# A hybrid diffusion block: the large GpSimd additions move to VectorE, and the inter-block weight is loaded instead of formed

## The chip, the cores and the metric

The kernel runs on one core of one Trainium2 chip, as one launch. The metric is device time in microseconds (us). The core has five instruction streams that run side by side and meet at semaphores: TensorE (PE in the profile; PEld is its weight load), VectorE (DVE), ScalarE (ACT), GpSimd (POOL) and SyncE (SP), which here issues nearly all DMA transfers. The order of instructions on each engine is fixed when the kernel is built: a scheduler takes the code's order as priority and puts out one list for each engine, so a change in the code can move rows far from it.

## What is computed

A sequence of 1024 latent tokens (width 1024), with 256 context tokens ahead of it as a prefix, goes through two kinds of recurrent heads in both directions, an output projection with a residual, and an expert-choice mixture of experts. Three parts of the reference matter for the change:

```python
# HGRN2 (4 heads): the key is 1 - f for each direction d
hg_k=[_to_heads(1.0 - f[:, :, d], HG_HEADS) for d in range(2)]

# mLSTM q and k: a 3x3 depthwise convolution over the 16 x 64 grid, then SiLU
y = lax.conv_general_dilated(t.reshape(B, rows, GRID_W, C), w[:, :, None, :], (1, 1), 'SAME', ...)
return jax.nn.silu(y + conv_b)

# mLSTM in chunks: weights within the chunk, and of the state that comes in
m_row = jnp.maximum(inter, jnp.max(d, axis=-1))
w_inter = jnp.exp(inter - m_row)
qk = jnp.einsum('bhid,bhjd->bhij', qc, kc) * jnp.exp(d - m_row[..., None])
num = jnp.einsum('bhij,bhjv->bhiv', qk, vc) + w_inter[..., None] * jnp.einsum('bhid,bhdv->bhiv', qc, c)
```

After the mixer, `v = rms_norm(xm) * (1 + scale) + shift` goes to the router and the experts. All arithmetic is float32 (products on TensorE are formed from two halves, high and low).

## The kernel before

The work is laid out in stages along the span. Until 215 us come the modulation, the context and HGRN2's values and gates; until some 460 us the four HGRN2 heads; until some 660 us output gates, the convolution, mLSTM values and the backward states; until some 900 us the eight blocks of 128 tokens of mLSTM outputs, mixer and router; then a sort that picks the tokens, and from 940 us the sixteen experts.

**HGRN2 (L640 to L711).** A head has two halves of 512 tokens. Features are on the partitions. L674 adds the two directions' keys on GpSimd (128x512, eight times); L347 on TensorE multiplies that sum with the queries; L675 forms the scaled queries of both directions on VectorE, and L363 scales the keys in the tree of levels.

**Convolution (L812 to L830).** A row r of 128 channels is one call of `conv(r)`, eight in all. L818 copies the projection into a padded tile, L821 forms the middle tap on ScalarE, L824 multiplies taps 3 and 5 on ScalarE and L825 adds each to the accumulator `cacc` on GpSimd. Six taps follow as L827 on VectorE. `silu2` (L502, L503) ends it, and the store to `d_qk` is issued by SP. Between these stand `back_k` (L842: load of keys, L480 to L486: transposed and scaled by `wkx`), `back_u` (L496 on TensorE, L386 on VectorE, store L853) and the modulation's sums (L295, L297), in the order of a list written out in the code:

```python
ORD = (5, 4, "v004", 6, "v044", 7, "v104", 0, "v144", "k7", 1, "u7", "k6", "k5", "u6", "k4", 2, "u5", 3,
       "o004", "u4", "k3", "o044", "u3", "k2", "u2", "o104", "k1", "M", "u1", "S0", "O0", "L0", "S1", "o144")
```

**Blocks (L932 to L952 and L1130 to L1180).** `scores(cc)` runs two blocks ahead of the mixer. SP loads `qkx` and then `MB` (L936): -M for eight head-directions, 128 numbers each, spread to all 128 partitions, 512 KB in 1024 pieces. Tiles `MB`, `E` and `qkx` have two buffers each. L943 (ScalarE, eight instructions) adds g to it and writes `E`; L944 (VectorE) takes the minimum with the causal mask; L945 is the exponent. GpSimd adds mu to `MB` in place (L946), ScalarE takes its exponent (L947), VectorE multiplies it with the queries (L950), and E with the scores from TensorE (L949). `outputs` (L957 to L982) uses both as stationary operands (L975 with E, L976 with MB). `mixed` loads `kin` and `go` (L1001, L1002) and forms `mix` (L1005, L1006). `mixer` loads `xm` (L1020), and L1027, L1028 add the residual. `router` forms the normalised row `vt`: L1052 to L1054, and L1055 adds the shift B2b on GpSimd (128x1024, eight times).

**Gates (`ml_gates`, L425 to L470).** It forms -M in one 128x128 tile and stores its two halves to `d_nm` in DRAM; `mu_b` is the copy of mu for L946, and `mcol` holds mu for each partition of that tile.

Of the kernel before, what the change touches and what calls it, by code (L numbers as in the profile page):

```python
# [9 lines left out]
F32 = mybir.dt.float32  # L10
# [5 lines left out]
AF = mybir.ActivationFunctionType  # L16
# [3 lines left out]
P = 128  # L20
# [12 lines left out]
def tile_hybrid_block(ctx, tc, x, c, cx, c_ctx, ada_w, ada_b, norm1_w, w_in, conv_w, conv_b,  # L33
# [6 lines left out]
    V, S, G, T = nc.vector, nc.scalar, nc.gpsimd, nc.tensor  # L40
# [12 lines left out]
    d_sb = dram.tile([8, P, 516], F32, name="d_sb")  # L53
    d_gx = dram.tile([16, 1024], F32, name="d_gx")
    d_nm = dram.tile([8, 1024], F32, name="d_nm")
    d_g = dram.tile([4, 1024], F32, name="d_g")
    d_v = dram.tile([1024, 1024], F32, name="d_v")
    d_acc = dram.tile([1024, 1024], F32, name="d_acc")
# [330 lines left out]
    def ml_gates(pool):  # L389
# [64 lines left out]
        V.tensor_scalar(M, M, -1.0, None, op0=OP.mult)  # L454
        for d in range(2):
            load(d_nm[4 * d:4 * d + 4].rearrange("h (c i) -> (h c) i", i=P), M[64 * d:64 * d + 32])
        pt = bank("ms")
        T.transpose(pt[:, 0:128], g, ident)
        T.transpose(pt[:, 128:256], b, ident)
# [3 lines left out]
        for d in range(2):  # L463
            V.tensor_copy(gT[:, :, d, :], xcol(0, d))
            S.activation(emn[:, :, d, :], xcol(128, d), AF.Exp, scale=-1.0)
            V.tensor_copy(mu_b[:, :, d, :], xst(0, d))
            V.tensor_sub(wkx[:, :, d, :], xcol(0, d), xst(80, d))
            V.tensor_sub(wsx[:, :, d, :], xst(0, d), xst(80, d))
            V.tensor_sub(wkc[:, :, d, :], view(pt, 64 * d + 32, [[1, 2], [2, 4]]), cst(80, d))
            V.tensor_sub(wsc[:, :, d, :], cst(0, d), cst(80, d))  # L470
# [105 lines left out]
    mlc = const.tile([P, 2, 4, 129], F32, name="mlc", tag="mlc", bufs=1)  # L576
    gT = const.tile([P, 8, 2, 4], F32, name="gT")
    emn = const.tile([P, 8, 2, 4], F32, name="emn")
    mu_b = const.tile([P, 8, 2, 4], F32, name="mu_b")
    wkx = const.tile([P, 8, 2, 4], F32, name="wkx")  # L580
    wsx = const.tile([P, 8, 2, 4], F32, name="wsx")
    wkc = const.tile([P, 2, 2, 4], F32, name="wkc")
# [65 lines left out]
    with tc.tile_pool(name="hgp", bufs=1) as hp_:  # L648
        tl = lambda name, shape, bufs: hp_.tile([P] + shape, F32, name=name, tag=name, bufs=bufs)
        fw = {}  # L650
        for h in range(4):
# [17 lines left out]
            for hf in range(2):  # L669
                f, qk = F[hf], QK[hf]  # L670
                K, Q = tl("hgK", [2, 512], 2), tl("hgQ", [2, 512], 3)
                A, U = tl("hgA", [4, P], 3), tl("hgU", [4, 2, P], 3)
                V.tensor_scalar(K, f, -1.0, 1.0, op0=OP.mult, op1=OP.add)
                G.tensor_add(qk[:, 1, :], K[:, 0, :], K[:, 1, :])  # L674
                V.tensor_mul(Q, qk[:, 0, :].unsqueeze(1).to_broadcast([P, 2, 512]), view(f, 512, [[-512, 2], [1, 512]]))  # L675
                dec = hg_tree(hp_, f, K, Q, qk, A)
                hg_u(hp_, K, lambda cc: hv[:, 4 * hf + cc, h * P:(h + 1) * P], U, ((0, 4 - hf), (1 - hf, 4)))
                Qs.append(Q), As.append(A), Us.append(U), decs.append(dec)
# [133 lines left out]
    def conv(r):  # L812
# [6 lines left out]
        acc = cvp.tile([P, 16, 64], F32, name="cacc", tag="cacc", bufs=2)  # L819
        tap = lambda t: view(pad, 65 * (t // 3) + t % 3, [[65, 16], [1, 64]])  # L820
        S.activation(acc, tap(4), AF.Identity, bias=convb[:, r:r + 1], scale=tapw(4, r))  # L821
        for t in (3, 5):
            one = cvp.tile([P, 16, 64], F32, name="cone", tag="cone", bufs=2)
            S.mul(one, tap(t), tapw(t, r))  # L824
            G.tensor_add(acc, acc, one)  # L825
        for t in (0, 1, 2, 6, 7, 8):
            V.scalar_tensor_tensor(acc, tap(t), tapw(t, r), acc, op0=OP.mult, op1=OP.add)  # L827
        res = cvp.tile([P, 1024], F32, name="cres", tag="cres", bufs=2)
        silu2(res, acc.rearrange("p r c -> p (r c)"))
# [101 lines left out]

    def scores(cc):  # L932

        qk, MB = tl("qkx", [8, P], 2), tl("MB", [8, P], 2)
        load(qk, d_qk[cc])
        load(MB, bass.AP(tensor=d_nm.tensor, offset=d_nm.offset + cc * P, ap=[[0, P], [1024, 8], [1, P]]))  # L936
        pq = bank("hg", [P, 4, P])
        for h in range(4):
            T.matmul(pq[:, h, :], qk[:, 4 + h, :], qk[:, h, :], start=True, stop=True)
        E = tl("E", [2, 4, P], 2)  # L940
        for d in range(2):
            for h in range(4):
                S.activation(E[:, d, h, :], MB[:, 4 * d + h, :], AF.Identity, bias=gT[:, cc, d, h:h + 1])  # L943
            V.tensor_tensor(E[:, d], E[:, d], cmask[:, d, :].unsqueeze(1).to_broadcast([P, 4, P]), op=OP.min)  # L944
        S.activation(E, E, AF.Exp)  # L945
        G.tensor_add(MB, MB, mu_b[:, cc].rearrange("p d h -> p (d h)").unsqueeze(2).to_broadcast([P, 8, P]))  # L946
        S.activation(MB, MB, AF.Exp)  # L947
        for d in range(2):
            V.scalar_tensor_tensor(E[:, d], pq, KSCALE, E[:, d], op0=OP.mult, op1=OP.mult)  # L949
            V.tensor_mul(MB[:, 4 * d:4 * d + 4, :], qk[:, 0:4, :], MB[:, 4 * d:4 * d + 4, :])  # L950
        kt = ml_k_tok(blk, lambda h: qk[:, 4 + h, :], wkx[:, cc, 0], False) if cc < 7 else None
        return E, MB, kt  # L952

# [93 lines left out]
    def router(cc, xm):  # L1047

        row = slice(cc * P, (cc + 1) * P)
        r2 = tb("r2", [1], 2)  # L1050
        vt = tb("vt", [1024])
        S.activation(vt, xm, AF.Square, scale=1.0 / 32, accum_out=r2)  # L1052
        rsqrt(r2, r2, 1)
        V.scalar_tensor_tensor(vt, xm, r2, A2b, op0=OP.mult, op1=OP.mult)  # L1054
        G.tensor_add(vt, vt, B2b)  # L1055
        kept["v"] = load(d_v[row], vt)
        if dbg and "xm" in dbg:
            nc.sync.dma_start(dbg["xm"][row], xm)
            nc.sync.dma_start(dbg["v"][row], vt)
        return r2  # L1060
# [389 lines left out]
```

## Time and profile before

| | |
|---|---|
| runs | 1557.04, 1558.73, 1561.94 us |
| median of the runs | 1558.73 us |
| the profiled execution, own time | 1559.33 us |
| the profiled execution, span of the core | 1557.6 us |
| PE, DVE, ACT, POOL busy | 1447.8, 1230.4, 864.7, 174.8 us |
| granted clock of TensorE, mean | 0.967 |
| chain that ended last | PE 64%, DVE 13%, DMA 10%, issue 6%, ACT 4%, POOL 2% |

The span is the stretch from the first to the last instruction of the core; the device time of the same execution is 1.7 us longer. A busy engine is not yet a bound: which wait ends last in a stage has to be read there. The chain of waits is followed back from the end, at each step to what released it. A timeline row gives the start, the length, the engine, the line, and in square brackets the idle time ahead of it with its releaser.

### The profile page before, as it was taken

To read this page: it belongs to the slowest core of one execution; us is meant where nothing else is said; L and a number is where in the kernel's file an instruction comes from. 1 tells how busy PE (TensorE), PEld (TensorE's weight loads), DVE (VectorE), ACT (ScalarE), POOL (GpSimd) and SP (SyncE) were. 2 spreads that over 40 slices of the span, in tenths; PEclk is the share of its full clock that TensorE was granted. 3 is DMA by queue.
4 is the path that set the end of the run, shared out by engine and by line. 5 is a ranking of instruction groups with operands and counts; after the bars stand their busy time and mean duration, and the time that the engine had idled before them with its cause. 6 is when DMAs were issued, how large, how long until landed. Compare 5 with 4: busy or idle time off the path is not lost.

```text
span 1557.6 us, 23134 instructions
## 1 busy us (share of the span) xinstructions
PE 1447.8 (93%) x8121; PEld 1206.9 (77%) x8121; DVE 1230.4 (79%) x2193; ACT 864.7 (56%) x1454; POOL 174.8 (11%) x136
## 2 busy tenths in 40 slices
PE   7999999999999998988888947999999999999996
PEld 2899878888898896977677735888888888888764
DVE  3685577888866859546757796999999999998887
ACT  3764424334434343345545315777787787777775
POOL 0000000000002221210222110010000000000003
PEclk9999999999999998989898977999999999999998
DMA  9741311220334254276753486999999999999942
GB/s 268 258 128 31 110 54 35 75 82 22 115 102 142 82 149 149 72 194 211 223 183 112 158 320 211 370 391 374 386 387 384 385 389 383 387 376 362 352 141 109
DMA packets 181201, 337.31 MB, mean 217 GB/s; under 512 B 13560, under 2 KB 108348, under 8 KB 181084
## 3 DMA queue, kind: packets, MB, share of 16 engines
q1 hardware_dynamic: 176472, 319.99, 58.0%
q0 software_dynamic: 4320, 15.73, 4.1%
q8 instruction: 64, 1.05, 0.3%
q14 instruction: 53, 0.43, 0.1%
q10 hardware_dynamic: 292, 0.10, 0.0%
HBM read 303.38 MB, written 32.39 MB: 216 GB/s over the span
## 4 chain that ended last, share of the span: by engine, by line
PE 64%; DVE 13%; DMA 10%; issue 6%; ACT 4%; POOL 2%; SPq 0%; ACTq 0%; POOLq 0%; DVEq 0%
PE mm L1303 22%; PE mm L278 11%; PE hg L1303 10%; PE mm L286 5%; PE hg L350 3%; DMA MB<-d_nm 3%; DVE cacc L827 3%; PE hg L215 2%; PE ms L1288 2%; DMA wraw<-in_w_in_dram 1%; PE mm L1026 1%; PE ms L382 1%; POOL cacc L825 1%; DMA wraw<-in_ada_w_dram 1%; PE mm L496 1%
## 5 line engine op out<-in xcount | busy, mean ns | idle before, releaser
L286 PE MATMUL mm<-whi,uh 128*128 128x256 f32 (+1 forms) x512 | 145.6, 284 | 3.0 <-DVE Sb L386 1.3
L286 PE MATMUL mm<-wlo,uh 128*128 128x256 f32 (+1 forms) x512 | 145.1, 283 | 0.0
L286 PE MATMUL mm<-whi,ul 128*128 128x256 f32 (+1 forms) x512 | 144.8, 283 | 0.0
L253 DVE TENSOR_TENSOR wlo<-wraw,whi 128x512 fp32r<-128x512 f32 x96 | 64.7, 686 | 49.5 <-ACT whi L252 49.0
L286 PEld LDWEIGHTS mm<-whi,uh 128*128 128x128 f32 x512 | 96.7, 189 | 5.2 <-DVE Sb L386 1.5
L286 PEld LDWEIGHTS mm<-whi,ul 128*128 128x128 f32 x512 | 96.8, 189 | 0.0
L286 PEld LDWEIGHTS mm<-wlo,uh 128*128 128x128 f32 x512 | 96.3, 188 | 0.3
L1303 PE MATMUL mm<-qkx,xT 128*128 128x512 f32 x256 | 83.7, 408 | 0.6 <-ACT xT L1289 0.3
L827 DVE SCALAR_TENSOR_TENSOR cacc<-pad,cols,cacc 128x1024 f32<-128x1024 f32 x48 | 63.6, 1325 | 24.4 <-POOL cacc L825 23.6
L1303 PE MATMUL mm<-E,xT 128*128 128x512 f32 x256 | 81.2, 398 | 0.4 <-ACT E L922 0.4
L1303 PE MATMUL mm<-MB,xT 128*128 128x512 f32 x256 | 80.8, 397 | 0.0
L252 ACT CAST whi<-wraw 128x512 fp32r<-128x512 f32 x96 | 58.4, 620 | 38.3 <-PE mm L278 24.8
L344 ACT COPY hgc<-hgK 128x512 f32<-128x512 f32 x56 | 35.5, 634 | 78.1 <-DVE hgK L363 38.6
L350 PE MATMUL hg<-hgQ,hgc 128*128 128x128 f32 x448 | 65.9, 291 | 1.0 <-DVE hgQ L366 1.0
L350 PEld LDWEIGHTS hg<-hgQ,hgc 128*128 128x128 f32 x448 | 57.8, 191 | 10.8 <-issue 6.9
L278 PE MATMUL mm<-uh,whi 128*128 128x512 f32 x192 | 63.4, 405 | 0.0
L278 PE MATMUL mm<-ul,whi 128*128 128x512 f32 x192 | 63.4, 404 | 0.0
L278 PE MATMUL mm<-uh,wlo 128*128 128x512 f32 x192 | 61.5, 399 | 0.0
L297 DVE SCALAR_TENSOR_TENSOR ac<-wraw,csil,ac 128x256 f32<-128x256 f32 x112 | 55.9, 499 | 4.1 <-DMA wraw<-in_ada_w_dram 2.2
L1303 PEld LDWEIGHTS mm<-E,xT 128*128 128x128 f32 x256 | 47.9, 189 | 13.7 <-ACT E L922 1.7
L1303 PEld LDWEIGHTS mm<-MB,xT 128*128 128x128 f32 x256 | 48.2, 188 | 11.9
L359 DVE COPY_PREDICATED hgA<-lm,hg 128x512 f32<-128x512 uint8 x56 | 41.4, 740 | 18.4 <-PE hg L350 17.1
(602 smaller groups left out, 4304.2 us busy)
## 6 DMA issues: line engine op xcount, KB each, us to landing
wraw<-in_w_in_dram SPq DMA_DIRECT2D x48, 512.0 KB
wl<-in_exp_w_up_dram SPq DMA_DIRECT2D x34, 512.0 KB
wh<-in_exp_w_up_dram SPq DMA_DIRECT2D x34, 512.0 KB
wh<-in_exp_w_gate_dram SPq DMA_DIRECT2D x34, 512.0 KB
wl<-in_exp_w_gate_dram SPq DMA_DIRECT2D x34, 512.0 KB
wraw<-in_ada_w_dram SPq DMA_DIRECT2D x32, 512.0 KB
wl<-in_exp_w_down_dram SPq DMA_DIRECT2D x29, 512.0 KB
wh<-in_exp_w_down_dram SPq DMA_DIRECT2D x29, 512.0 KB
```

The source lines that it names most:

```text
L215: T.matmul(pm[0:2, :256], csil[:, k, :], adas[i, k // 4][:, k % 4, :, :], start=(k == 0), stop=(k == 7))
L252: S.copy(hi[:, :, cs], src)
L253: V.tensor_sub(lo[:, :, cs], src, hi[:, :, cs])
L278: T.matmul(o, l, r[:, k, i * n:(i + 1) * n], start=(k == 0 and q == 0), stop=(k == 7 and q == 2))
L286: T.matmul(o, l[:, k, ts], r, start=(k == 0 and q == 0), stop=(k == 7 and q == 2))
L297: V.scalar_tensor_tensor(ac, a2[:, k % 4, :], csil[:, k, 0:1], ac, op0=OP.mult, op1=OP.add)
L344: S.copy(view(kc, 0, [[h, 2], [2 * h, 256 // h], [1, h]]), view(K, 0, [[512 + h, 2], [2 * h, 256 // h], [1, h]]))
L350: T.matmul(pb[:, cc, :], kc[:, cc * P:(cc + 1) * P], view(Q, cc * P, pat), start=True, stop=True)
L359: V.copy_predicated(A, lmask[h].unsqueeze(1).to_broadcast([P, 4, P]), scores(h))
L827: V.scalar_tensor_tensor(acc, tap(t), tapw(t, r), acc, op0=OP.mult, op1=OP.add)
L1288: T.transpose(pt[:, k, :], view(src, 4 * q + k, [[8, P]]), ident)
L1303: T.matmul(o, l[:, k, :], r[:, 512 * j:512 * j + 512], start=(k == 0 and p_ == 0), stop=(k == 7 and p_ == 2))
```

## The change

1. `conv`: taps 3 and 5 are no longer multiplied on ScalarE and added on GpSimd. All eight taps are the same VectorE instruction.
2. HGRN2: the keys' sum of L674 is on VectorE.
3. `router`: the shift's addition of L1055 is on VectorE.
4. `scores`: exp(mu - M) is taken once, in `ml_gates`, from the 128x128 tile (its partition's mu is the bias), and stored to a new DRAM tensor `d_em` by two more stores. In each block -M is loaded into E itself, where L943 and the rest work in place, and MB is loaded from `d_em`, a second spread load of 512 KB, issued right behind the first. The addition of mu (L946), the exponent (L947) and `mu_b` are gone. In the code, MB's product now stands ahead of E's.

Later lines move up by 1 to 3: L827 becomes L826, L944 L943, L950 L946, L949 L947, L1006 L1003, L1027 and L1028 L1024 and L1025.

```diff
@@ ml_gates
             load(d_nm[4 * d:4 * d + 4].rearrange("h (c i) -> (h c) i", i=P), M[64 * d:64 * d + 32])
+        em = mk("gem")
+        S.activation(em, M, AF.Exp, bias=mcol)
+        for d in range(2):
+            load(d_em[4 * d:4 * d + 4].rearrange("h (c i) -> (h c) i", i=P), em[64 * d:64 * d + 32])
@@
-            V.tensor_copy(mu_b[:, :, d, :], xst(0, d))
@@ HGRN2
-                G.tensor_add(qk[:, 1, :], K[:, 0, :], K[:, 1, :])
+                V.tensor_add(qk[:, 1, :], K[:, 0, :], K[:, 1, :])
@@ conv
-        for t in (3, 5):
-            one = cvp.tile([P, 16, 64], F32, name="cone", tag="cone", bufs=2)
-            S.mul(one, tap(t), tapw(t, r))
-            G.tensor_add(acc, acc, one)
-        for t in (0, 1, 2, 6, 7, 8):
+        for t in (0, 1, 2, 3, 5, 6, 7, 8):
             V.scalar_tensor_tensor(acc, tap(t), tapw(t, r), acc, op0=OP.mult, op1=OP.add)
@@ scores
-        qk, MB = tl("qkx", [8, P], 2), tl("MB", [8, P], 2)
+        qk, MB, E = tl("qkx", [8, P], 2), tl("MB", [8, P], 2), tl("E", [2, 4, P], 2)
         load(qk, d_qk[cc])
-        load(MB, bass.AP(tensor=d_nm.tensor, offset=d_nm.offset + cc * P, ap=[[0, P], [1024, 8], [1, P]]))
+        for t, src in ((E.rearrange("p d h t -> p (d h) t"), d_nm), (MB, d_em)):
+            load(t, bass.AP(tensor=src.tensor, offset=src.offset + cc * P, ap=[[0, P], [1024, 8], [1, P]]))
@@
-        E = tl("E", [2, 4, P], 2)
         for d in range(2):
             for h in range(4):
-                S.activation(E[:, d, h, :], MB[:, 4 * d + h, :], AF.Identity, bias=gT[:, cc, d, h:h + 1])
+                S.activation(E[:, d, h, :], E[:, d, h, :], AF.Identity, bias=gT[:, cc, d, h:h + 1])
@@
-        G.tensor_add(MB, MB, mu_b[:, cc].rearrange("p d h -> p (d h)").unsqueeze(2).to_broadcast([P, 8, P]))
-        S.activation(MB, MB, AF.Exp)
         for d in range(2):
+            V.tensor_mul(MB[:, 4 * d:4 * d + 4, :], qk[:, 0:4, :], MB[:, 4 * d:4 * d + 4, :])
             V.scalar_tensor_tensor(E[:, d], pq, KSCALE, E[:, d], op0=OP.mult, op1=OP.mult)
-            V.tensor_mul(MB[:, 4 * d:4 * d + 4, :], qk[:, 0:4, :], MB[:, 4 * d:4 * d + 4, :])
@@ router
-        G.tensor_add(vt, vt, B2b)
+        V.tensor_add(vt, vt, B2b)
```

**SP's queue in the block stage.** These are loads and stores in the order in which SP issues them, around the scores of blocks 2 and 3 (`d_acc`, `d_v` are stores, `wor`, `v` expert weights). Before:

```order
166 L936 DMA MB<-d_nm 128x8x128
167 L1020 DMA xm<-in_x_dram 128x1024
168 L1056 DMA d_v<-vt 128x1024
169 L1001 DMA kin<-d_hg 128x512
170 L1002 DMA go<-d_go 128x1024
171 L892 DMA v_7417<-in_exp_w_gate_dram 128x1024
172 L935 DMA qkx<-d_qk 128x1024
173 L936 DMA MB<-d_nm 128x8x128
```

After:

```order
174 L936 DMA E<-d_nm 128x8x128
175 L936 DMA MB<-d_em 128x8x128
176 L1017 DMA xm<-in_x_dram 128x1024
177 L1053 DMA d_v<-vt 128x1024
178 L998 DMA kin<-d_hg 128x512
179 L999 DMA go<-d_go 128x1024
180 L891 DMA v_7383<-in_exp_w_gate_dram 128x1024
181 L934 DMA qkx<-d_qk 128x1024
182 L936 DMA E<-d_nm 128x8x128
183 L936 DMA MB<-d_em 128x8x128
```

The second spread load stands between the first one and xm, kin and go.

**VectorE at the scores of the last block.** Rows of the mask (`E<-E,cmask`), of MB's product and of the mixer before it (`mm`, `xm`, `mix`). Before:

```order
965 L1006 SCALAR_TENSOR_TENSOR mix<-go,hsum 128x512
966 L1027 TENSOR_TENSOR mm<-mm,g1b 128x512
967 L944 TENSOR_TENSOR E<-E,cmask 128x512
968 L1028 TENSOR_TENSOR xm<-xm,mm 128x512
969 L944 TENSOR_TENSOR E<-E,cmask 128x512
970 L950 TENSOR_TENSOR MB<-qkx,MB 128x512 x2
971 L1027 TENSOR_TENSOR mm<-mm,g1b 128x512
972 L1028 TENSOR_TENSOR xm<-xm,mm 128x512
```

After:

```order
963 L943 TENSOR_TENSOR E<-E,cmask 128x512
964 L946 TENSOR_TENSOR MB<-qkx,MB 128x512 x2
965 L1024 TENSOR_TENSOR mm<-mm,g1b 128x512
966 L1003 SCALAR_TENSOR_TENSOR mix<-go,hsum 128x512
967 L1025 TENSOR_TENSOR xm<-xm,mm 128x512
968 L943 TENSOR_TENSOR E<-E,cmask 128x512
969 L1024 TENSOR_TENSOR mm<-mm,g1b 128x512
970 L1025 TENSOR_TENSOR xm<-xm,mm 128x512
```

MB's two products have moved ahead of the second mask, of `mix` and of both halves of the residual.

## Rows read from the trace of the kernel before

**Rows 1.** The page's part 2: the span in 40 equal slices of 39 us, busy tenths of TensorE and VectorE.

```profile
PE   7999999999999998988888947999999999999996
DVE  3685577888866859546757796999999999998887
```

**Rows 2.** Four stretches: from:to and length in us, busy time of PE, PEld, DVE, ACT and POOL (x instructions), granted clock of TensorE, DMA share, GB/s.

```profile
584.00:623.00 39.00, 32.08 (x147) 25.59 (x146) 35.75 (x53) 12.30 (x22) 4.70 (x2) 0.87 0.46 149
...
740.00:780.00 40.00, 33.15 (x191) 28.02 (x190) 30.09 (x85) 20.94 (x61) 11.23 (x7) 0.87 0.69 217
...
880.00:940.00 60.00, 32.58 (x171) 25.23 (x169) 55.47 (x262) 12.51 (x32) 8.84 (x6) 0.79 0.72 264
940.00:1557.00 617.00, 592.62 (x2752) 475.32 (x2752) 569.18 (x632) 464.91 (x572) 56.46 (x48) 0.98 0.91 339
```

**Rows 3.** The chain that ended last, at the end of the convolution: start, length in us, what.

```profile
625.70 1.05 ACT cone L824
...
644.31 2.40 POOL cacc L825
646.74 1.29 DVE cacc L827
...
653.49 1.29 DVE cacc L827
...
657.14 3.21 DMA d_qk<-cres
...
670.69 13.44 DMA MB<-d_nm
```

**Rows 4.** The same chain in the block stage.

```profile
750.24 13.40 DMA MB<-d_nm
...
774.70 9.75 DMA MB<-d_nm
784.47 1.57 ACT E L943 x5
...
792.07 1.29 DVE MB L950 x2
...
829.34 10.47 DMA MB<-d_nm
839.84 2.46 ACT E L943 x8
842.37 2.44 POOL MB L946
844.83 1.06 ACT MB L947
845.92 1.29 DVE MB L950 x2
```

**Rows 5.** GpSimd's groups of instructions: line, operation, tiles, shapes, count, then busy us and mean ns of one, then idle time ahead and what ended it.

```profile
L825 POOL TENSOR_TENSOR cacc<-cacc,cone 128x1024 f32<-128x1024 f32 x16 | 39.1, 2445 | 132.2 <-ACT cone L824 131.6
...
L1055 POOL TENSOR_TENSOR vt<-vt,B2b 128x1024 f32<-128x1024 f32 x8 | 19.0, 2373 | 16.3 <-DVE vt L1054 11.5 <-DVE den L979 4.8
L946 POOL TENSOR_TENSOR MB<-MB,mu_b 128x1024 f32<-128x1024 f32 x8 | 17.7, 2208 | 84.5 <-ACT E L943 77.0 <-PE ms L1011 7.5
...
L674 POOL TENSOR_TENSOR hgqk<-hgK 128x512 f32<-128x512 f32 x8 | 14.0, 1768 | 283.9 <-DVE hgqk L667 283.9
```

**Rows 6.** VectorE's groups, different shapes apart, in the same columns.

```profile
L297 DVE SCALAR_TENSOR_TENSOR ac<-wraw,csil,ac 128x256 f32<-128x256 f32 x112 | 55.9, 499 | 4.1 <-DMA wraw<-in_ada_w_dram 2.2
L363 DVE TENSOR_TENSOR hgK<-hgK,hgT 128x512 f32<-128x512 f32 x48 | 32.8, 683 | 0.0
...
L923 DVE TENSOR_TENSOR mlc<-wl,v 128x1024 fp32r<-128x1024 f32 x25 | 30.5, 1218 | 0.8 <-ACT v L922 0.7
```

**Rows 7.** The timeline of three stretches: of all engines from 600 us, of VectorE and then of GpSimd from 215 us, and of VectorE near 830 us.

```profile
601.41 2.53 DVE L295 TENSOR_SCALAR ac<-wraw,csil 128x256 f32<-128x256 f32 x1 [0.25 <-DMA wraw<-in_ada_w_dram]
...
601.44 4.77 POOL L825 TENSOR_TENSOR cacc<-cacc,cone 128x1024 f32<-128x1024 f32 x2 [18.73 <-ACT cone L824]
...
603.98 4.08 DVE L297 SCALAR_TENSOR_TENSOR ac<-wraw,csil,ac 128x256 f32<-128x256 f32 x4
...
608.47 0.77 PE L496 MATMUL mm<-v,mkt 128*128 128x129 f32 x2 [5.27 <-DVE mkt L486]
...
216.21 1.97 DVE L675 TENSOR_TENSOR hgQ<-hgqk,hgf 128x1024 f32<-128x1024 f32 x1
218.11 1.76 DVE L363 TENSOR_TENSOR hgK<-hgK,hgf 128x512 f32<-128x512 f32 x1
219.79 1.21 DVE L675 TENSOR_TENSOR hgQ<-hgqk,hgf 128x1024 f32<-128x1024 f32 x1
...
830.24 2.12 DVE L978 TENSOR_TENSOR den<-den,emn 128x2 f32<-128x2 f32 x2
```

**Rows 8.** Waits from 215 to 460 us: engine and line, what it waited for, us in total, times, longest.

```profile
PE hg L347 <- POOL hgqk L674: 2.9, 4, 0.8
```

**Rows 9.** The timeline of ScalarE: the first L943 of block 0 and of block 1, whose loads were issued at 664.05 and 670.69 us.

```profile
676.82 1.86 ACT L943 ACTIVATE E<-MB,gT 128x128 f32<-128x128 f32 x6 [7.73 <-DMA d_go<-gsg]
...
684.16 0.69 ACT L943 ACTIVATE E<-MB,gT 128x128 f32<-128x128 f32 x2 [1.04 <-DMA MB<-d_nm]
```

**Rows 10.** Waits from 670 to 940 us, as in rows 8.

```profile
ACT E L943 <- DMA MB<-d_nm: 30.5, 7, 7.3
```

More of the change, by code (lines that the diff above doesn't have):

```diff
@@ L55, in tile_hybrid_block @@
     d_nm = dram.tile([8, 1024], F32, name="d_nm")
+    d_em = dram.tile([8, 1024], F32, name="d_em")
     d_g = dram.tile([4, 1024], F32, name="d_g")
@@ L578, in tile_hybrid_block @@
     emn = const.tile([P, 8, 2, 4], F32, name="emn")
-    mu_b = const.tile([P, 8, 2, 4], F32, name="mu_b")
     wkx = const.tile([P, 8, 2, 4], F32, name="wkx")
```

## The prediction

> **What bounds the kernel now.** I read the page's slices first, because a mean hides stages. TensorE is at nine tenths or more in most slices; the reader should see the dip in slice 16 (584 to 623 us), the eights from 662 us on and the hole at 880 to 940 us [rows 1]. The same stretches in numbers: in the last 617 us TensorE works 592.62 us and the DMA engines 0.91 of the time, so nothing that the change touches sets that stage; it only starts when the stage ahead of it is done. At 584 to 623 us VectorE is busy 35.75 of 39 us, and at 880 to 940 us 55.47 of 60: there VectorE is the bound [rows 2]. Then I read the chain that ended last. At the end of the convolutions it runs through GpSimd's additions and ScalarE's multiplication in front of them, a store, a vector load, and so to the first spread loads MB [rows 3]. In the block stage it runs three more times through an MB load, issued at 750.24, 774.70 and 829.34 us [rows 4].
>
> **What goes and what comes, in busy time.** GpSimd loses 39.1 + 19.0 + 17.7 + 14.0 = 89.8 us [rows 5]. ScalarE loses 16 multiplications of 1.05 us (17 us) and eight exponents of 1.06 us [rows 3, 4]. VectorE gets 16 taps at 1.29 us [rows 3] = 20.6, eight 128x512 additions at 0.683 [rows 6] = 5.5 and eight 128x1024 additions at 1.218 [rows 6] = 9.7: 35.8 us more. It also gets time back: where a GpSimd addition runs, a VectorE instruction with two inputs lasts until it ends. In head 0 one L675 takes 1.97 us and the next 1.21, and an L363 takes 1.76 us against 0.683; near 830 us two L978 on two columns take 2.12 us; near 602 us an L295 and the L297 after it end with the two GpSimd additions [rows 6, 7]. Four heads at 0.76 + 1.08 us are 7.4 us; the two at 602 us, against 0.5 us each (L297's mean is 499 ns [rows 6]), are 4.1; some 1.8 us for each block's router addition are 14. That is an estimate of 25 us. VectorE's busy time should so rise by about 11 us net: little, if what is removed lies on the path and what is added does not.
>
> **HGRN2 keys (L674).** TensorE's L347 waits four times for the GpSimd sum, 2.9 us in all [rows 8]. On VectorE the sum takes 0.683 instead of 1.3 to 2.3 us and stands ahead of L675. TensorE is full there otherwise. I take -2 us; bounds -3 (all the wait and none of the new work felt) and +3 (eight sums ahead of L675 show half of their 5.5).
>
> **Convolutions, middle.** At 601.44 two GpSimd additions start and take 4.77 us; L295 and L297 end with them, the key scaling L486 stands behind, and TensorE's L496 idles 5.27 us until 608.47 [rows 7]. That stall was the lock's. But VectorE is at 92% of this stretch [rows 2], and each row of the convolution now brings it 2.6 us more, so half comes back as queueing ahead of L486. I take -2 us; bounds -7 (all of it, and a little of the lowered clock of 0.87 in that stretch [rows 2]) and +3 (the extra taps of two rows, 5.2 us, against the 4.1 us of lock, with the rest falling in front of L486 at the wrong time).
>
> **Convolutions, end.** From 625.70 us, where ScalarE's L824 starts, to the end of the last tap at 654.78 the chain takes 29.1 us: two rows of six taps each, with ScalarE's L824 and GpSimd's L825 ahead of each row's taps [rows 3]. Sixteen taps in a row at 1.31 us are 21 us, so the last d_qk store goes out about 7 us earlier by this count. TensorE has other work meanwhile, so this is worth nothing by itself until the first MB loads: SP stands behind that store, and the second block's MB load is issued at 670.69, 13 us behind the start of that store [rows 3]. I take 6 us of the 7 as reaching the first two loads. There the second spread load takes it away again (next paragraph): block 0's two loads and block 1's E now queue, E of block 1 one load later than MB was, 7.3 - 6 = about +1, with GpSimd's and one exponent's time out of the path behind it. I take -3; bounds -6 and +5 (none of the 6 arrives, and the 7.3 shows but for what TensorE can do meanwhile).
>
> **Blocks: what leaves.** After each MB load comes ScalarE's L943, then GpSimd's L946, L947 and the product L950. In the last block: L943 at 839.84, L946 at 842.37 for 2.44 us, L947 at 844.83, L950 at 845.92 [rows 4]. The locks of L1055 on the router's and the outputs' small operations go, and eight exponents of ScalarE. I take -6 us over eight blocks, of which the lock of one router addition (1.8 us) falls on the path in about three; bounds -9 and -3.
>
> **Blocks: what the second load costs.** The new d_em load is as large and has the same form as the first. Its price is the distance between two such loads of which the second was issued while the first was still under way: L943 of block 0 starts at 676.82 and of block 1, still idle for its load, at 684.16, so 7.3 us [rows 9]. MB's exponent hence comes 7.3 us after E's input. Before, L950 came 845.92 - 839.84 = 6.1 us after the landing in the last block, and 792.07 - 784.47 = 7.6 us in an earlier one [rows 4]. So the new MB is +1.2 and -0.3 us against the old: nearly even. But in the new order the product stands ahead of the mixer's last steps, ahead of the second masked minimum and ahead of E's own product, which can wait for MB now, and xm, kin and go stand behind the second load on SP. I take +5 us, 1.7 for each of the three loads of the chain; bounds 0 (everything behind it has slack) and +24, in the rival below.
>
> A sentence on the notes: the Trainium skill, DMA: Bandwidth & Descriptors, Specifications, gives 512 bytes as the smallest transfer that still runs at line rate, and each piece here has 512 bytes. By that rule the second load would be cheap: 0.52 MB at the 339 GB/s that the expert stretch moves [rows 2] are 1.5 us. The trace's 7.3 us speak against it for this load, which reads each address 128 times; I go by the trace and keep the rule as the last rival.
>
> **Router additions (L1055) in the sort.** At 880 to 940 us VectorE is the bound [rows 2]. Two of the eight additions fall there, 2 x 1.22 us more, and two GpSimd additions of 2.4 us go that blocked VectorE for most of their time. I take 0; bounds -2 and +2.5.
>
> **Sum.** -2 - 2 - 3 - 6 + 5 + 0 = -8 us on the profiled execution's 1559.33 us: 1551.3. The median of the runs is 0.6 us lower, which I leave: the forecast is 1551, in its own case 1545 to 1554.
>
> **Rivals.** *The second load takes over the path.* It decides where the d_em load lands more than about 6 to 7.6 us after d_nm's, or where the product that waits for it holds VectorE's queue for mask, mixer and E. Then each of the three loads of the chain costs 6 us (7.3 less the 1.3 that I called nearly even) instead of 1.7, and the start of the blocks, with four spread loads in a row instead of two, loses 6 where I had a gain of 3. From -8 that is 13 us more for the loads and 9 more for the start: +14, or 1573; I take 3 off where a stall of one block hides that of another: 1570, within 1563 and 1576, slower than before. For it: L943 idles 30.5 us on MB's landing already now, and DMA engines carry 0.69 of the time at 740 to 780 us [rows 2, 10]. Against it: at 740 to 780 us TensorE has 6.85 of 40 us idle [rows 2], room for some of it, and the last row of the convolution is done earlier.
>
> *VectorE fills.* The additions fall where VectorE is the bound (584 to 623 and 880 to 940 us) and only head gaps and blocks gain: -2 for the heads, +1 for the middle, -1 at the end, -6 + 6 in the blocks: -2, that is 1557, no change. For it: 55.47 of 60 us busy. Against it: the lock time that goes is nearly as long as what comes.
>
> *Spread loads run near line rate side by side.* If the two loads overlap because they read two tensors, E and MB land together, the block term is 0 instead of +5 and the start gains its full 6: -8 - 5 - 3 = -16, 1543. The only pair in the trace speaks against it [rows 9].
>
> **How the numbers follow.** Forecast (1551) 0.38; second load on the path (about 1570) 0.31; VectorE fills (1557) 0.23; loads side by side (1543) 0.08. The bound of what a measurement can tell is 0.3%, 4.7 us: below 1554 counts as faster, above 1563.4 as slower. Of the first case 0.03 lies above 1554; of the third 0.04 lies below it and 0.02 above 1563.4; of the second 0.02 lies within. Faster 0.35 + 0.04 + 0.08 = 0.47; same 0.03 + 0.02 + 0.17 = 0.22; slower 0.29 + 0.02 = 0.31. The range for 8 in 10 takes the two outer cases in but for their tails (some 0.03 below and 0.1 above): 1540 to 1573.
>
> **What would show it right or wrong.** Right: no VectorE two-input operation above its usual length in the HGRN2, convolution and block stages; L496 near 608 us waits 3 us or less; the last cres ends about 6 us earlier; the distance from E's to MB's landing is 7 us, and TensorE's idle time between 700 and 860 us is no larger than before. Wrong: DMA MB<-d_em leads the chain where MB<-d_nm did, with VectorE idle in front of its product L946 by more than 10 us in all; or the stretch from 584 to 623 us gets longer with VectorE full; or the idle time of L943 falls far under 30 us because both loads land at once.

## The result, and the profile after

The changed kernel takes 1579.26 us (median of four runs, 1578.73 to 1582.25) against 1558.52 us: ratio 1.0134, 95% interval 1.0113 to 1.0155. It is slower by some 21 us, where 1551 us was forecast and 1573 us was the upper end of the range. The profiled execution took 1582.25 us, its span is 1580.4 us.

The slices answer to [rows 1]; a slice is now 39.5 us:

```profile
PE   7999999999999999868676965999999999999996
DVE  3685477888768788447545796999999999998887
```

The dip of TensorE at 584 to 623 us is gone, and the block stage has sixes and sevens where there were eights. The same in numbers, to be read beside [rows 2] (from:to, length, busy PE, PEld, DVE, ACT and POOL, granted clock, DMA share, GB/s):

```profile
584.00:623.00 39.00, 36.77 (x175) 29.46 (x174) 33.55 (x56) 11.39 (x20) 0.00 (x0) 1.00 0.44 142
...
660.00:700.00 40.00, 21.14 (x154) 19.74 (x153) 13.09 (x40) 12.98 (x38) 0.00 (x0) 0.79 0.66 131
...
740.00:780.00 40.00, 24.05 (x125) 19.84 (x123) 18.96 (x52) 15.67 (x47) 2.12 (x3) 0.79 0.76 173
...
900.00:960.00 60.00, 33.25 (x177) 26.02 (x175) 55.80 (x267) 12.62 (x33) 2.27 (x4) 0.81 0.72 264
960.00:1580.00 620.00, 594.88 (x2754) 476.95 (x2754) 570.37 (x632) 465.48 (x573) 57.01 (x48) 0.98 0.91 337
```

At 584 to 623 us TensorE works 4.7 us more than before and its granted clock is 1.00 instead of 0.87. At 740 to 780 us it works 9.1 us less. The experts take as long as before. So the additions gave something and the blocks took more than that.

The chain through the blocks answers to [rows 4]; these are its pieces that are loads (start, length in us):

```profile
654.70 10.23 DMA E<-d_nm
666.36 15.29 DMA E<-d_nm
690.94 10.93 DMA E<-d_nm
739.34 18.56 DMA MB<-d_em
761.55 18.62 DMA sb<-d_sb
788.22 19.94 DMA MB<-d_em
818.25 15.66 DMA MB<-d_em
847.01 17.52 DMA MB<-d_em
```

MB loads of 15.7 to 19.9 us stand where loads of 9.8 to 13.4 us stood, four against the three of [rows 4], and three loads of E and one of sb stand beside them. The waits from 640 to 960 us, the first block's included (engine, line and releaser, us in total, times, longest), answer to [rows 10]:

```profile
DVE E L943 <- ACT E L942: 46.4, 8, 12.3
ACT E L942 <- DMA E<-d_nm: 44.6, 7, 8.4
DVE MB L946 <- DMA MB<-d_em: 36.7, 7, 7.0
ACT E L944 <- DVE E L943: 28.4, 7, 6.7
```

ScalarE waits 44.6 us for E's load, where it waited 30.5 us for MB's. What is new is the third row, VectorE in front of MB's product, and the last one: E's exponent (L944) waits 28.4 us for the masked minimum, where the kernel before had

```profile
ACT E L945 <- DVE E L944: 3.4, 5, 0.8
```

One block shows why. ScalarE has E's input at 749.82. On VectorE:

```profile
751.13 0.69 DVE L943 TENSOR_TENSOR E<-E,cmask 128x512 f32<-128x512 f32 x1 [5.06 <-ACT E L942]
757.93 0.69 DVE L946 TENSOR_TENSOR MB<-qkx,MB 128x512 f32<-128x512 f32 x1 [6.10 <-DMA MB<-d_em]
758.54 0.68 DVE L943 TENSOR_TENSOR E<-E,cmask 128x512 f32<-128x512 f32 x1
759.14 0.69 DVE L946 TENSOR_TENSOR MB<-qkx,MB 128x512 f32<-128x512 f32 x1
...
760.34 1.29 DVE L947 SCALAR_TENSOR_TENSOR E<-hg,E 128x512 f32<-128x512 f32 x2
```

The second mask needs nothing from MB, but stands behind MB's product, which waits 6.10 us for its load. It stands so in four of the eight blocks, and E's own product stands behind MB's in all eight (in five of eight before). SP's issues in the same block (start, length of the issue):

```profile
737.68 0.33 SPq L1026 DMA_DIRECT2D d_acc<-xm  x1
...
738.53 0.72 SPq L936 DMA_DIRECT2D E<-d_nm  x1
739.34 1.77 SPq L936 DMA_DIRECT2D MB<-d_em  x1
741.16 4.63 SPq L1017 DMA_DIRECT2D xm<-in_x_dram  x1
745.88 1.91 SPq L1053 DMA_DIRECT2D d_v<-vt  x1
747.84 3.75 SPq L998 DMA_DIRECT2D kin<-d_hg  x1
751.65 2.35 SPq L999 DMA_DIRECT2D go<-d_go  x1
...
761.55 5.81 SPq L956 DMA_DIRECT2D sb<-d_sb  x1
```

Most issues take 0.3 to 0.4 us, as the first row. The four behind the two spread loads take 1.9 to 4.6 us each, and sb's, behind the next pair (not shown), 5.8: SP itself is held, and all that it has to issue comes later.

The part that was forecast as a gain is there too. VectorE's groups, to be read beside [rows 6, 7]:

```profile
L678 DVE TENSOR_TENSOR hgQ<-hgqk,hgf 128x1024 f32<-128x1024 f32 x8 | 9.8, 1221 | 0.0
L1052 DVE TENSOR_TENSOR vt<-vt,B2b 128x1024 f32<-128x1024 f32 x8 | 9.7, 1214 | 0.0
...
L364 DVE TENSOR_TENSOR hgK<-hgK,hgf 128x512 f32<-128x512 f32 x8 | 5.5, 688 | 0.0
L677 DVE TENSOR_TENSOR hgqk<-hgK 128x512 f32<-128x512 f32 x8 | 5.5, 687 | 0.0
...
L975 DVE TENSOR_TENSOR den<-den,emn 128x2 f32<-128x2 f32 x32 | 4.2, 155 | 4.8 <-ACT den L974 4.7
```

In the kernel before, the first, the third and the last of these groups were

```profile
L675 DVE TENSOR_TENSOR hgQ<-hgqk,hgf 128x1024 f32<-128x1024 f32 x8 | 12.6, 1572 | 0.0
...
L363 DVE TENSOR_TENSOR hgK<-hgK,hgf 128x512 f32<-128x512 f32 x8 | 9.8, 1224 | 0.0
...
L978 DVE TENSOR_TENSOR den<-den,emn 128x2 f32<-128x2 f32 x32 | 9.5, 321 | 1.9 <-ACT den L977 1.7
```

L678's mean falls from 1572 to 1221 ns, L364's from 1224 to 688 and L975's from 321 to 155, and the two moved additions cost 687 and 1214 ns, as estimated. VectorE's busy time is 1231.1 us, 0.7 us above before, where 11 us more were estimated: its other instructions became shorter by nearly all that the additions cost now. In the heads that was the GpSimd addition (e9 below, with the keys' sum alone moved, has 1220 and 684 ns for the first two of these); the rest is not split by cause.

### The profile page after: what moved, and what is told of

It is laid out like the page before. It is cut to its first block, busy times and chain, and to the rows that moved or that the text cites. A ratio compares the mean times of both kernels' runs of the same rounds, so it can differ in the third digit from the quotient of the medians.

```text
span 1580.4 us, 23097 instructions
## 1 busy us (share of the span) xinstructions
PE 1443.7 (91%) x8121; PEld 1202.8 (76%) x8121; DVE 1231.1 (78%) x2223; ACT 841.8 (53%) x1431; POOL 85.6 (5%) x96
## 3 DMA queue, kind: packets, MB, share of 16 engines
q8 instruction: 64, 1.05, 0.3%
## 4 chain that ended last, share of the span: by engine, by line
PE 74%; DMA 11%; DVE 8%; issue 4%; ACT 2%; POOL 1%; SPq 0%; ACTq 0%; POOLq 0%; DVEq 0%
PE mm L1300 21%; PE mm L279 14%; PE mm L287 11%; PE hg L1300 10%; DMA MB<-d_em 5%; PE hg L351 4%; DMA E<-d_nm 2%; PE hg L216 2%; PE ms L1285 2%; DMA sb<-d_sb 1%; PE ms L383 1%; PE mm L1023 1%; PE mm L500 1%; PE hg L1390 1%; PE mm L972 1%
## 5 line engine op out<-in xcount | busy, mean ns | idle before, releaser
L826 DVE SCALAR_TENSOR_TENSOR cacc<-pad,cols,cacc 128x1024 f32<-128x1024 f32 x64 | 81.8, 1281 | 14.3 <-ACT cacc L824 13.5
```

## The experiments

Each ratio is to runs of the kernel before on the same chip, with its 95% interval.

| run | what | median us | ratio | interval |
|---|---|---|---|---|
| e9_keys_only | keys' sum alone | 1548.15 | 0.9949 | 0.9931 to 0.9968 |
| e7_taps_only | taps alone | 1545.62 | 0.9943 | 0.9921 to 0.9964 |
| e8_shift_only | shift alone | 1554.98 | 1.0004 | 0.9992 to 1.0016 |
| e1_adds_only | the three together | 1540.24 | 0.9895 | 0.9868 to 0.9922 |
| e2_weights_only | part 4 alone | 1592.94 | 1.0237 | 1.0215 to 1.0259 |
| (the change) | all four | 1579.26 | 1.0134 | 1.0113 to 1.0155 |
| e3_product_behind | all, product later in the code | 1574.89 | 1.0111 | 1.0086 to 1.0136 |
| e13_product_held_back | all, product later on VectorE | 1564.50 | 1.0047 | 1.0030 to 1.0063 |
| e12_four_dmas_one_copy | all, loads in four | 1549.90 | 0.9954 | 0.9937 to 0.9971 |
| e6_four_copies | all, loads in four, four copies | 1544.94 | 0.9943 | 0.9924 to 0.9963 |
| e14_pieces_of_1kb | all, 1 KB pieces 8 KB apart | 1567.89 | 1.0070 | 1.0054 to 1.0087 |
| e15_pieces_1kb_apart | all, 512-byte pieces 1 KB apart | 1508.98 | 0.9688 | 0.9672 to 0.9705 |
| e16_rows_of_4608_bytes | all, 512-byte pieces 4.5 KB apart | 1509.63 | 0.9696 | 0.9678 to 0.9714 |
| e4_block_major | all, one piece of 4 KB | 1508.11 | 0.9692 | 0.9670 to 0.9714 |
| e5_adds_one_big_load | additions, one load, one piece of 4 KB | 1505.20 | 0.9686 | 0.9664 to 0.9709 |
| e11_layout_only | the kernel before, one piece of 4 KB | 1527.24 | 0.9815 | 0.9788 to 0.9843 |

### Which part costs

**e1_adds_only** takes part 4 of the change back, **e2_weights_only** takes parts 1 to 3 back. Edit of the second (the first is the change's own diff for `ml_gates` and `scores`, reversed):

```diff
-                V.tensor_add(qk[:, 1, :], K[:, 0, :], K[:, 1, :])
+                G.tensor_add(qk[:, 1, :], K[:, 0, :], K[:, 1, :])
-        for t in (0, 1, 2, 3, 5, 6, 7, 8):
+        for t in (3, 5):
+            one = cvp.tile([P, 16, 64], F32, name="cone", tag="cone", bufs=2)
+            S.mul(one, tap(t), tapw(t, r))
+            G.tensor_add(acc, acc, one)
+        for t in (0, 1, 2, 6, 7, 8):
-        V.tensor_add(vt, vt, B2b)
+        G.tensor_add(vt, vt, B2b)
```

> Parts 1 to 3 of the change alone (taps, keys and shift on VectorE); the weights are formed from one load as before. Theory A (the second spread load costs the time, the three moves of additions gain): 1545 to 1552 us, and TensorE's busy share from 584 to 623 us as high as in the changed kernel (36.8 of 39 us). Theory B (the added VectorE work and the new order cost the time): 1565 us or more. Theory C (both cost a part): 1556 to 1565 us.

> Part 4 alone (two spread loads, no formed weight); taps, keys and shift as before. Theory A: 1578 to 1592 us, the whole loss and what the moved additions gave back. Theory B: within 1553 to 1563 us. Theory C: 1566 to 1576 us.

Measured: the additions gain 1.05%, 16 us, more than theory A had; part 4 alone loses 2.37%, 37 us, just above its range. The two add up: 0.9895 x 1.0237 = 1.0130, the change's own ratio. Theory B is out. The stage can be read from one line of VectorE, MB's product, which comes twice in each block: its first and last start. Before, in the changed kernel, and with the additions alone:

```profile
L950 DVE TENSOR_TENSOR MB<-qkx,MB x16: 681/685/693, 683.1 to 846.5; 128x512 f32<-128x512 f32 x16
```

```profile
L946 DVE TENSOR_TENSOR MB<-qkx,MB x16: 673/686/693, 672.5 to 867.6; 128x512 f32<-128x512 f32 x16
```

```profile
L946 DVE TENSOR_TENSOR MB<-qkx,MB x16: 671/684/693, 666.9 to 828.5; 128x512 f32<-128x512 f32 x16
```

The changed kernel enters the blocks 10.6 us earlier and needs 195 us from the first product to the last instead of 163. With the additions alone it enters 16.2 us earlier and needs 162; with part 4 alone it enters at 683.4 us, as before, and needs 194.

**e7_taps_only, e8_shift_only and e9_keys_only** are the kernel before with one part of the change each; their lines in this order:

```diff
+        for t in (0, 1, 2, 3, 5, 6, 7, 8):
...
+        V.tensor_add(vt, vt, B2b)
...
+                V.tensor_add(qk[:, 1, :], K[:, 0, :], K[:, 1, :])
```

> Only the taps of part 1 on VectorE, the rest as before. The prediction put the middle and the end of the convolutions at -5 us together. Theory A (the gain of parts 1 to 3, some 16 us, is the taps' chain and the stall at 600 us): 1542 to 1549 us. If most of that gain is in the heads and blocks instead: 1551 to 1557 us.

> Only the shift of part 3 on VectorE, the rest as before. The prediction put its lock at some 2 us in three blocks and nothing in the sort. If so: 1549 to 1554 us. If VectorE in the sort pays for it: 1557 to 1562 us.

> Only the keys' sum of part 2 on VectorE, the rest as before. The prediction put it at -2 us (bounds -3 and +3). If that is right: 1552 to 1554 us. If the moves are additive, taps 9 us and the three together 16, the shift nothing: 1547 to 1550 us, and the rest of the gain would lie in a stage that the keys don't touch, by another order of instructions.

Taps gain 0.57% (9 us), keys 0.51% (8 us), the shift nothing: 0.9943 x 0.9949 x 1.0004 = 0.9896, what the three give together. The shift lies above the range for its own theory and below the one for a cost. The keys are the surprise: the last of TensorE's products that read the sum starts at 422.2 us instead of 426.1, so 4 us are gained in the heads. The first MB product starts at 676.8 us, 6.3 us ahead of the kernel before, so some of the rest is gained between the heads and the blocks, by what was not separated.

### The place of the waiting product

**e3_product_behind** puts MB's products behind both of E's in the code:

```diff
         for d in range(2):
-            V.tensor_mul(MB[:, 4 * d:4 * d + 4, :], qk[:, 0:4, :], MB[:, 4 * d:4 * d + 4, :])
             V.scalar_tensor_tensor(E[:, d], pq, KSCALE, E[:, d], op0=OP.mult, op1=OP.mult)
+        for d in range(2):
+            V.tensor_mul(MB[:, 4 * d:4 * d + 4, :], qk[:, 0:4, :], MB[:, 4 * d:4 * d + 4, :])
```

> All four parts, but in the code MB's product stands behind E's own product. If the cost is the place of the waiting product on VectorE (it holds mask, mixer and E's product): 1560 to 1568 us. If the cost is the second load on the queue and its late landing, wherever the product stands: 1575 to 1581 us.

Its 1.0111 tells nothing of the order: on all five engines the instructions stand as in the changed kernel. The scheduler puts the product in the same place, wherever the code has it. So this run is a second measurement of the change (the intervals overlap). **e13_product_held_back** forces the order:

```diff
-            V.tensor_mul(MB[:, 4 * d:4 * d + 4, :], qk[:, 0:4, :], MB[:, 4 * d:4 * d + 4, :])
-            V.scalar_tensor_tensor(E[:, d], pq, KSCALE, E[:, d], op0=OP.mult, op1=OP.mult)
+            ep = V.scalar_tensor_tensor(E[:, d], pq, KSCALE, E[:, d], op0=OP.mult, op1=OP.mult)
+        with tc.issue_after(ep.ins):
+            for d in range(2):
+                V.tensor_mul(MB[:, 4 * d:4 * d + 4, :], qk[:, 0:4, :], MB[:, 4 * d:4 * d + 4, :])
```

> All four parts with uncut loads of 512-byte pieces, and MB's products now held behind E's products on VectorE by an explicit order; the loads and their issue are as in the changed kernel. In the run with the product behind in the code alone, VectorE's rows came out in the same order as in the changed kernel, so it told nothing of the order; here they do not. If the place of the waiting product, which holds mask, mixer and E, is what the four-DMA run took away: 1545 to 1560 us. If what helped there was the cut, or the loads' landing itself is the cost: 1570 us or more.

1.0047: between the two expectations. Its waits from 640 to 960 us:

```profile
ACT E L942 <- DMA E<-d_nm: 51.1, 8, 8.8
DVE E L943 <- ACT E L942: 35.3, 7, 12.7
ACT E L944 <- DVE E L943: 7.4, 5, 3.4
DVE MB L949 <- DMA MB<-d_em: 3.3, 3, 1.4
```

The two new waits of the change are nearly gone (36.7 to 3.3 and 28.4 to 7.4 us), and the wait for E's load stays. The order is worth (1.0134 - 1.0047) / (1.0134 - 0.9895) = 36% of the loss; by the intervals it is a quarter to a half, and with e3's 1.0111 in place of 1.0134 it is 30%. This edit didn't move VectorE's rows alone: the scheduler also issued two of the eight pairs of loads, and some of xm, d_acc and d_v, at other places in SP's queue, against what was expected of it. So the share is that of the order with these moves; what is left stands with the loads.

### What makes a load slow

**e4_block_major** stores both small tensors block by block, so that each partition reads 4 KB in one piece:

```diff
-    d_nm = dram.tile([8, 1024], F32, name="d_nm")
-    d_em = dram.tile([8, 1024], F32, name="d_em")
+    d_nm = dram.tile([8, 8, P], F32, name="d_nm")
+    d_em = dram.tile([8, 8, P], F32, name="d_em")
...
-        for t, src in ((E.rearrange("p d h t -> p (d h) t"), d_nm), (MB, d_em)):
-            load(t, bass.AP(tensor=src.tensor, offset=src.offset + cc * P, ap=[[0, P], [1024, 8], [1, P]]))
+        for t, src in ((E.rearrange("p d h t -> p (d h t)"), d_nm), (MB.rearrange("p k t -> p (k t)"), d_em)):
+            load(t, bass.AP(tensor=src.tensor, offset=src.offset + cc * 1024, ap=[[0, P], [1, 1024]]))
```

> All four parts, but both small tensors in DRAM lie block by block, so that a load reads 4 KB in one piece for each partition (128 pieces in place of 1024, the same 512 KB). If a load's 7 us come from its 1024 pieces: each lands in 2 to 3 us, the loss is gone and the kernel takes 1538 to 1552 us. If they come from the bytes or from 128 partitions reading the same addresses: 1575 to 1582 us.

0.9692, 48 us faster than before and below the expectation: the loss is gone and another 32 us with it. VectorE's masks, products and mixer steps in the block stage stand in the order of the changed kernel; with loads that land early this order costs little (E's exponent waits 4.8 us for the mask in e16 below, which has the same lists of instructions, where it waited 28.4). The same line of VectorE as above:

```profile
L946 DVE TENSOR_TENSOR MB<-qkx,MB x16: 673/685/693, 658.8 to 794.1; 128x512 f32<-128x512 f32 x16
```

The products span 135 us instead of 195. That is not yet the cause: number of pieces, their size, their distance, and how many partitions read one address are all candidates. Five runs tell them apart.

**e6_four_copies** stores the tensors four times and cuts a load into four DMAs of 32 partitions, each from its own copy; **e12_four_dmas_one_copy** cuts in the same way and reads one copy (r * 8192 left out):

```diff
-            load(t, bass.AP(tensor=src.tensor, offset=src.offset + cc * P, ap=[[0, P], [1024, 8], [1, P]]))
+            for r in range(4):
+                load(t[32 * r:32 * r + 32], bass.AP(tensor=src.tensor, offset=src.offset + r * 8192 + cc * P, ap=[[0, 32], [1024, 8], [1, P]]))
```

> All four parts with pieces of 512 bytes, but the two small tensors are stored four times and each load is four DMAs of 32 partitions, each from its own copy; 1024 pieces for a load as in the change, every address read by 32 partitions instead of 128, and 48 more issues on SP. If the load is slow because many partitions read the same addresses: 1512 to 1545 us, with a load in 2 to 4 us. If it is slow because of its number of pieces: 1575 us or more.

> All four parts, each spread load cut into four DMAs of 32 partitions as in the run with four copies, but all from the same copy. If the reading of the same addresses by many partitions makes the load slow: 1575 us or more (the cut alone gives nothing). If it was the cut that helped: 1540 to 1555 us.

The first alone would have spoken for the readers of one address; the control gives nearly the same (intervals overlap), so it isn't that. The cut made the scheduler place E's products and masks ahead of MB's product and spread the issues, so these two mix order and loads. Why the cut gains 15 us more than e13 stays open.

**e14_pieces_of_1kb** lays two heads' rows together: 512 pieces of 1 KB, 8 KB apart. **e15_pieces_1kb_apart** keeps 1024 pieces of 512 bytes, but 1 KB apart. **e16_rows_of_4608_bytes** keeps the layout of the change and pads each row by 512 bytes. Their lines, in this order (d_em, the views of the tiles and the stores follow suit):

```diff
+    d_nm = dram.tile([4, 8, 2, P], F32, name="d_nm")
+            load(t, bass.AP(tensor=src.tensor, offset=src.offset + cc * 256, ap=[[0, P], [2048, 4], [1, 256]]))
```

> All four parts; the small tensors lie so that two heads' rows are together: a spread load is 512 pieces of 1 KB, 8 KB apart, in place of 1024 of 512 bytes, 4 KB apart. If the number of pieces sets a load's time: a load takes half as long (about 4 us) and the kernel 1520 to 1550 us. If the distance of the pieces sets it: as slow as the change, 1570 us or more.

```diff
+    d_nm = dram.tile([8, 8, 2 * P], F32, name="d_nm")
+            load(t, bass.AP(tensor=src.tensor, offset=src.offset + cc * 2048, ap=[[0, P], [2 * P, 8], [1, P]]))
```

> All four parts; 1024 pieces of 512 bytes as in the change, but the eight pieces of a partition lie 1 KB apart instead of 4 KB. If the number and size of the pieces set a load's time: 1570 to 1582 us. If their distance does (pieces far apart meet in the same part of the memory): 1505 to 1535 us.

```diff
+    d_nm = dram.tile([8, 1152], F32, name="d_nm")
+            load(t, bass.AP(tensor=src.tensor, offset=src.offset + cc * P, ap=[[0, P], [1152, 8], [1, P]]))
```

> All four parts; the layout of the small tensors is that of the change but each row is padded from 4096 to 4608 bytes, so the eight pieces of 512 bytes lie 4.5 KB apart. If a multiple of 4 KB between the pieces makes the load slow: 1505 to 1525 us, as with 1 KB between them. If it is the wide spread of the pieces: 1570 us or more.

e14 stays slow with half the pieces (1.0070; its 1568 us lie 2 us below what distance alone had been expected to give), e15 and e16 are fast with all of them (0.9688 and 0.9696). e4, e14, e15 and e16 have the same list of instructions on each of the five engines, and in the blocks VectorE's is that of the change: between them only the shape of the small tensors and the addresses that loads and stores use differ. The waits from 640 to 960 us for the two loads, in e14 and then in e16, against 44.6 and 36.7 us in the changed kernel:

```profile
ACT E L942 <- DMA E<-d_nm: 43.0, 7, 9.6
...
DVE MB L946 <- DMA MB<-d_em: 27.3, 6, 6.2
```

```profile
ACT E L942 <- DMA E<-d_nm: 8.0, 6, 3.7
...
DVE MB L946 <- DMA MB<-d_em: 0.3, 1, 0.3
```

The DMA view of some microseconds that hold a pair of loads and parts of other transfers, in the changed kernel (741 to 758 us), in e14 (784 to 800) and in e15 (747 to 753); the pair's 2048 pieces (1024 in e14) are among the packets under 2 KB:

```profile
DMA packets 2286, 1.81 MB, mean 107 GB/s; under 512 B 52, under 2 KB 2100, under 8 KB 2286
```

```profile
DMA packets 1286, 1.89 MB, mean 118 GB/s; under 512 B 56, under 2 KB 1078, under 8 KB 1285
```

```profile
DMA packets 2292, 1.84 MB, mean 306 GB/s; under 512 B 52, under 2 KB 2100, under 8 KB 2292
```

2286 packets need 17 us in the change and 2292 alike need 6 us in e15. Pieces that lie 4 or 8 KB apart are slow, pieces that lie 1 or 4.5 KB apart are fast: the cause is their distance, by these four a multiple of 4 KB, and not their number, their size or the width of the spread. Other distances, such as 2 KB, were not tried. Half the pieces, or 8 KB in place of 4, gain some 10 us of the 70 between the changed kernel and e15. The Trainium skill, DMA: Bandwidth & Descriptors, Latency and other measured facts, tells of copies whose rate falls as the row pitch grows through large powers of two (its figures: 207 GB/s at 512 KiB, 103 at 4 MiB) and of 4 KiB of padding that restores it, with aliasing of memory channels as an inference; here something like it is seen at 4 KB, and 512 bytes of padding restore it. The mechanism behind it isn't shown here either.

### What the kernel before loses by it, and whether the weight is worth loading

**e11_layout_only** changes nothing in the kernel before but the layout of its one load; **e5_adds_one_big_load** has parts 1 to 3 with that load, and forms the weight on GpSimd and ScalarE as before. The load's line (d_nm's shape and its stores follow suit):

```diff
-        load(MB, bass.AP(tensor=d_nm.tensor, offset=d_nm.offset + cc * P, ap=[[0, P], [1024, 8], [1, P]]))
+        load(MB.rearrange("p k t -> p (k t)"), bass.AP(tensor=d_nm.tensor, offset=d_nm.offset + cc * 1024, ap=[[0, P], [1, 1024]]))
```

> The kernel before with nothing changed but the layout of the small tensor, so that its one spread load reads 4 KB for each partition. If the loss and the gain of the loads are as in the runs with cheap loads (e1 to e5: 35 us): 1518 to 1528 us. If that gain needs the moved additions as well: 1530 to 1545 us.

> Parts 1 to 3, and the weights formed from one load as before (GpSimd adds mu, ScalarE takes the exponent), but that load reads block by block, 4 KB for each partition. It tells whether loading the weight is worth anything once a load is cheap. If the loss of the change was the load alone and forming the weight costs little: 1506 to 1512 us, as with two block-major loads. If forming the weight costs what I put down for what leaves the blocks (6 us) or more: 1513 to 1525 us.

The layout alone gives 29 us; with the additions moved, 50 us. e5 and e4 agree within their intervals (0.9686 and 0.9692): with cheap loads, loading the weight is worth nothing that can be told from forming it. These versions, with e15 and e16, beat both kernels.

A third buffer for E and MB, which would let their loads start earlier, was not tried.

## Why the prediction was wrong

- **What bounds the kernel:** right. The loss lies in the block stage, on the chain of spread loads that [rows 4] had shown, and the expert stage only starts later.
- **HGRN2 keys, -2 us:** the sign was right, the size small: 8 us (5 to 11). I had priced TensorE's wait of 2.9 us alone. In e9 L363 and L675 are shorter, as above, and the last product that reads the sum starts 4 us earlier; where the other half is gained stays open.
- **Convolutions, -2 and -3 us:** taps alone gain 9 us (6 to 12). In the changed kernel the last tap starts 15 us earlier, and with taps alone too (638.3 us), where I had counted 7 from the last two rows (and 29.1 less 21 is 8); the taps' line in the kernel before and after, with the durations (min/median/max, ns) and the first and last start:

```profile
L827 DVE SCALAR_TENSOR_TENSOR cacc<-pad,cols,cacc x48: 1266/1283/3408, 501.2 to 653.5; 128x1024 f32<-128x1024 f32 x48
```

```profile
L826 DVE SCALAR_TENSOR_TENSOR cacc<-pad,cols,cacc x64: 1265/1284/1289, 492.9 to 638.6; 128x1024 f32<-128x1024 f32 x64
```

  No tap lasts 3408 ns any more, the first starts 8 us earlier, and from the first start to the last 64 taps take 146 us where 48 took 152. TensorE's wait of 5.27 us near 603 us is gone with its lowered clock, without the queueing that I had put against it. No run separates the middle from the end.
- **Shift, 0 in the sort, and its lock part of -6 us in the blocks:** together they were worth nothing (1.0004, within some 2 us). No run splits the two; the lock's share of the -6 isn't found.
- **Blocks, what leaves, -6 us:** not found. The shift gives nothing, and e5 against e4 shows that the formed weight (GpSimd's addition, ScalarE's exponent) costs nothing that can be measured when loads are early: some 4 us more would lie outside the intervals. What it costs behind the slow load no run prices by itself.
- **Blocks, the second load, +5 us: this is the step that failed.** Part 4 costs 37 us. The distance of the two landings came out near the forecast (7.3; in the block shown 749.82 to 757.93 is 8.1), with some luck: the first of the two rows that I read it from names d_go's store as its releaser, and not the load [rows 9]. What I did with it was wrong twice. I wrote that MB is "nearly even" and charged 1.7 us for each of three loads, though I had seen the new order of VectorE: holding mask and E's product behind the wait is about a third of the loss (e13, with the moves on SP). And I priced a late landing where a queue was filled: two loads at some 8 us each fill 16 of a block's 28 us (195 over the seven steps from the first block to the last), SP's issues behind them take up to 5.8 us each, and E's loads (44.6 us of waits) and sb come late as well. The rival "the second load takes over the path" had the mechanism and the point at which it decides, with 0.31. Its size did not come about as it was added up: it charged the start of the blocks 6 us where the changed kernel enters them 10.6 us earlier, and counted the chain's three loads and not all eight pairs; that its 1570 (up to 1576) is near 1579 is in part luck.
- **The rule of 512 bytes (the Trainium skill, DMA: Bandwidth & Descriptors, Specifications):** I set it aside because the trace showed 7.3 us for a load. The trace was right for this load, and e15 agrees with the rule: its stretch with 512-byte pieces runs at 306 GB/s, near the 339 of the experts. What I took for a property of the spread read ("reads each address 128 times") was the 4 KB between the pieces. Had I asked why the load in the kernel before was slow, I would have found 29 us there.
- **What was to show it wrong** did show it: VectorE idle in front of L946 for 36.7 us where more than 10 was the mark, and MB<-d_em in the lead of the chain.

## What to carry to other kernels

A transfer that is far slower than its bytes warrants is a finding before it is a price: ask what its addresses have in common (here pieces 4 KB apart, cured by 512 bytes of padding) before a change adds a second one. Charge a new load with the whole time that it takes of its queue, in each round and to all that is issued behind it, not with the lateness of the one tile that it brings. And where a scheduler sets the order, look whether an instruction that will wait stands ahead of work that need not: moving the line in the code may change nothing.

## What the hardware showed that was not expected

- 1024 reads of 512 bytes into 128 partitions take some 8 us when a partition's eight pieces lie 4 KB apart; a stretch with a pair of loads moves 107 GB/s in the changed kernel, and 306 GB/s with as many packets when the pieces lie 1 KB apart. 1 KB pieces 8 KB apart are slow as well (118 GB/s), rows padded to 4.5 KB are not (0.9696 of the time before).
- SP's issue of a DMA isn't always free: 0.3 to 0.4 us in most cases, and 1.9 to 5.81 us behind the slow loads of the block shown. Quick loads of as many pieces can hold SP too: in e16 one issue right behind such a pair takes 3.21 us.
- VectorE did 35.8 us of added work with 0.7 us more busy time (1231.1 against 1230.4): its other instructions became shorter by nearly as much, where I had collected 25 us from rows. For L363 and L675 e9 shows that it was the GpSimd addition; for the others it is likely and not shown.
